# Grouping the transposes and value products of the differential heads in a macaron layer's token mixer

## The chip, the cores and the metric

The kernel runs on one core of one Trainium2 chip. The metric is the time of one execution in microseconds on the device; below it is the median of three runs. One further execution was taken with the hardware profiler. Engines are named as in the profile: PE (TensorE, matrix products), PEld (its weight loads), DVE (VectorE), ACT (ScalarE), POOL (GpSimd) and SP (SyncE, which issues transfers).

## The reference, cut to what matters

A layer of 512 positions and width 1024: half a feed forward, a token mixer, half a feed forward, each behind an RMS norm and added to the input. Half of the mixer's width belongs to four differential heads; the other half to eight dilated heads. The change touches the differential ones:

```python
def diff_attention(q, k, v, lam, bias_table):
    ...
        s = jnp.einsum('bhmqd,bhmkd->bhmqk', q_blk, k).astype(jnp.float32) * scale
        dist = (start + jnp.arange(Q_BLOCK))[:, None] - k_pos[None, :]
        bias = table[t5_bucket(dist)].transpose(2, 0, 1).reshape(H, 2, Q_BLOCK, S)
        s = jnp.where(dist >= 0, s + bias, -jnp.inf)
        p = jax.nn.softmax(s, axis=-1)
        a = p[:, :, 0] - lam * p[:, :, 1]
        return jnp.einsum('bhqk,bhkd->bhqd', a, v32)
...
    oa = diff_attention(qa, ka, va, lam, rel_bias[:, :2 * N_DIFF_HEADS])
    oa = rmsnorm(oa, subln_gain) * (1.0 - lam0)
```

Each differential head has two query/key maps of width 64 and one value of width 128. The queries are taken in four rows of 128; row `i` sees `i + 1` blocks of 128 keys. The second map's probabilities, weighted, are subtracted from the first's, and the result times the values goes through an RMS norm of its own.

## The kernel before, in words

The mixer's order on PE, DVE and ACT is written out by the program itself. The frame is the projections: `plan` lists them (`q0 v0 q1 v1 q2 q3 q4 v2 q5 q6 v3 q7`), each cut into eight chunks. A `q` chunk is six products of 128 x 512 (a slice of the query and key projections of one pair of heads or one head), a `v` chunk twelve of 128 x 256 (values for two heads at a time). Chunk number `t` is called step `t`. `put(t, rank, f)` hangs a piece of attention work on a step: pieces of rank below 10 are issued before that step's chunk, in the order of their ranks, the others behind it. After that, one split of a weight (high part on ACT, low part on DVE) is taken from a list. Nothing is reordered afterwards on these three engines: an instruction that waits holds up everything behind it on its engine.

`attention(u, s)` hangs up one unit of work. Units 0 to 3 are the differential heads, starting at steps 12, 29, 45 and 53; units 4 to 7 are pairs of dilated heads, starting at 61, 77, 85 and 99. For a differential head:

- `score(m, i)` at step s + 2i + m (rank 6): two PE passes into a bank of the tag `s` (two buffers), a DVE instruction that adds the bias strip and takes the extreme (L1061), and `exp` on ACT (L1064).
- `combine(i)` at s + 2i + 3 (rank 5): reciprocal, factor and the weighted sum of the two maps on DVE (L1068 to L1075). It leaves row `i` of the probabilities in `pr`.
- `turn(0, i)` at tv + 2i (rank 2): `i + 1` transposes on PE (L1127) into a bank of the tag `t` (two buffers) and an ACT copy (L1130) into `ptb` (two buffers). Here tv is s + 5 or the step at which the head's values are projected, whichever is later: 17, 34, 50, 58.
- `values(0, i)` at tv + 2i + 2 (rank 1): `i + 1` products (L1139), two records each, into `po`, one of four banks of the tag `mm`, which the projections use too.
- From e = tv + 9 (26, 43, 59, 67): `squares` (e, rank 7; a small DVE instruction and four squares on ACT, L1147), `mean` (e + 1, rank 7; `f` and its successor on DVE, L1155 and L1156), four pieces of an inverse root by Newton steps (e + 2 and e + 3, rank 8, DVE), `scale` (e + 4, rank 7; DVE, L1161 and L1162), `finish` (e + 6, rank 3; four transposes on PE into a bank of the tag `t`, L1168, and an ACT copy), `finish_low` (e + 7, rank 8; the split `ml` on DVE, L1182).

For a dilated unit, `turn_part` (L1094, copy L1105) turns pieces of both maps into a tile of the tag `tx` (one buffer, 3072 columns); rows are scaled by `combine` (L1080 and L1084) at s + 2i + 3, the last at s + 2i + 2. The tag `tx` belongs to the input of the feed forwards outside the mixer and to the dilated units 4 to 6 within it.

What a query projection leaves in its banks is read by DVE (`tq` and `tk`, L970 and L972) and split again by ACT and DVE (L982 to L1008).

Of the kernel before, what the change touches and what calls it, by code (L numbers as in the profile page):

```python
# [14 lines left out]
F32 = mybir.dt.float32  # L15
# [6 lines left out]
P = 128  # L22
S = 512
# [5 lines left out]
NQ = S // P  # L29
# [25 lines left out]
HS = S // 2  # L55
# [4 lines left out]
OFF = [0, 128, 384, 768]  # L60
# [3 lines left out]
def tile_macaron(ctx: ExitStack, tc, xs, xT, wf, wgu1, wst1, wd1, wdg1, wqk, wv, wo, wgu2, wst2, wd2,  # L64
                 wdg2, lams, relb, onehot, addc, out):
    nc = tc.nc
    V, A, G, T = nc.vector, nc.scalar, nc.gpsimd, nc.tensor
# [4 lines left out]
    tp = ctx.enter_context(tc.tile_pool(name="tp", bufs=2))  # L72
    wp = ctx.enter_context(tc.tile_pool(name="wp", bufs=3))
    sp = ctx.enter_context(tc.tile_pool(name="sp", bufs=4))
    pp = ctx.enter_context(tc.tile_pool(name="pp", bufs=4, space=PSUM))
# [5 lines left out]
    def mm_bank(nm):  # L81
        return pp.tile([P, S], F32, tag="mm", name=nm, bufs=4)
# [8 lines left out]
    ident = cp.tile([P, P], F32, tag="ident", name="ident")  # L91
# [642 lines left out]
    with tc.manual_schedule(engines={mybir.EngineType.DVE, mybir.EngineType.Activation}):  # L734
        for t in range(4):
            raw = wp.tile([P, 1024], F32, tag="raw", name=f"raw_f{t}")
            h, l = w_place()
            for kk in range(2):
                k = 2 * t + kk
# [23 lines left out]
                if k > 1:  # L763
                    add_square(k - 1)
                tiles = [(heads[j][i], kk * 512 + (2 * j + i) * P)
                         for j in range(2) for i in range(2)]
                if k == 0:
                    for wx, xx in ((h, early[0]), (h, early[1]), (l, early[0])):
                        for ps, o in tiles:
                            T.matmul(ps[:], wx[:, o:o + P], xx[0][:],  # L770
                                     start=wx is h and xx is early[0], stop=False)
# [99 lines left out]
    v_end = [8 * plan.index(f"v{u // 2}") + 8 for u in range(8)]  # L871
    at = {}

    def put(t, rank, f, *a):
        at.setdefault(t, []).append((rank, f, a))
# [39 lines left out]
    vt = {}  # L915
# [123 lines left out]
    def attention(u, s):  # L1039
        diff, quick = u < 4, u == 7  # L1040
        st = {}
# [78 lines left out]
                             skip_group_check=True)  # L1120
                n += w

        def turn(m, i):
            w = (i + 1) * P
            pt = pp.tile([P, S], F32, tag="t", name=f"pt{u}{m}{i}", bufs=2)
            for k in range(i + 1):
                T.transpose(pt[:, k * P:(k + 1) * P],  # L1127
                            st["pr"][m][:, OFF[i] + k * P:OFF[i] + (k + 1) * P], ident[:])
            ptb = tp.tile([P, S], F32, tag="ptb", name=f"ptb{u}{m}{i}", bufs=2)
            A.copy(ptb[:, :w], pt[:, :w])  # L1130
            st["ptb", m, i] = ptb

        def values(m, i):
            if "po" not in st:
                st["po"] = mm_bank(f"po{u}")
                st["po3"] = st["po"][:].rearrange("p (i d) -> p i d", i=NQ)
            fo = (u % 4) * P
            for k in range(i + 1):
                T.matmul(st["po3"][:, i, :], st["ptb", m, i][:, k * P:(k + 1) * P],  # L1139
                         vt[0, k][:, fo:fo + P], start=k == 0, stop=k == i)  # L1140

        def squares():
            ob_ = tp.tile([P, S], F32, tag="ob", name=f"ob{u}")
# [51 lines left out]
            put(s + step * i + (1 if quick else 3 if diff or i < 3 else 2),  # L1195
                5 if diff or quick or i != 2 else 6.5, combine, i)
        if diff:
            tv = max(s + 5, v_end[u])
            for i in range(NQ):
                put(tv + 2 * i, 2, turn, 0, i)  # L1200
                put(tv + 2 * i + 2, 1, values, 0, i)
            e = tv + 9
            put(e, 7, squares)
            put(e + 1, 7, mean)
            for j in range(4):
                put(e + 2 + j // 2, 8, lambda j=j: st["rs"][j]())
            put(e + 4, 7, scale)
            put(e + 6, 3, finish)
            put(e + 7, 8, finish_low)
        elif quick:  # L1210

            for j, part in enumerate((((0, 0, 3),), ((1, 1, 3), (2, 2, 3)),
                                      tuple((k, 3, 4) for k in range(NQ)))):
                for m in range(2):
                    put(s + 4 + j, 2, turn_part, m, part)
                put(s + 5 + j, 1, values_part, part)
            put(s + 7, 3, finish)
            put(s + 7, 4, finish_low)
        else:
            tv = max(s + 9, v_end[u])  # L1220
            parts = ((0, 0, 4),), ((1, 1, 4),), ((2, 2, 4), (3, 3, 4))
            for j, part in enumerate(parts):
                for m in range(2):
                    put(tv + j, 2, turn_part, m, part)
                put(tv + 4, 1, values_part, part)
            put(tv + 5, 3, finish)
            put(tv + 5, 8, finish_low)

    for w in plan:
        chunks += (qk_chunks if w[0] == "q" else v_chunks)(int(w[1]))  # L1230
        if w[0] == "q":
            attention(int(w[1]), len(chunks) + (4 if w[1] == "0" else 3 if w[1] == "7" else 5))
# [336 lines left out]
```

## Time and profile before

| what | value |
|---|---|
| median of three runs | 931.54 us (931.29 to 931.55) |
| the profiled execution | 932.39 us |
| its span, first to last instruction | 930.6 us |
| mean granted TensorE clock | 0.999 |
| copies of turned probabilities, L1130 | 16, of 255 to 591 ns, median 427 |

The profile gives one execution. The differential heads' attention lies between about 360 and 483 us of the span, the rest of the mixer and the feed forwards around it. In a timeline each row is the start in us, the length in us, the engine, the line, the operation, the tile written and the tiles read, the shape, the count of instructions merged into the row, and in brackets the idle time before it with the instruction that ended it. `L1061` is line 1061 of the kernel before. A length on PE is that of a record, whose end overlaps its successor.

### The profile page before, as it was taken

What the parts mean: (1) busy time and instruction counts of PE and PEld (TensorE: products, weight loads), DVE (VectorE), ACT (ScalarE), POOL (GpSimd) and SP (SyncE); (2) the same over time, 40 slices, a digit from 0 to 9 for tenths busy, and PEclk for the clock granted to TensorE, in tenths of its full rate; (3) what the DMA queues carried; (4) which work ended last, traced back from release to release, by engine and by line L of the source; (5) the groups of instructions that cost most, each with busy time, mean ns of one, the idle gap of its engine ahead of it and who ended that gap; (6) DMA issues with size and microseconds to landing.
All of it is one profiled execution on the core that took longest, in us unless ns stands there. A gap on an engine that the chain in (4) does not pass through costs nothing.

```text
span 930.6 us, 17116 instructions
## 1 busy us (share of the span) xinstructions
PE 922.9 (99%) x6402; PEld 854.7 (92%) x6402; DVE 727.9 (78%) x1504; ACT 543.5 (58%) x1122; POOL 98.3 (11%) x117
## 2 busy tenths in 40 slices
PE   9999999999999999999999999999999999999997
PEld 8888999999999999988979778889999999999997
DVE  7797887677888897668876556797888777888784
ACT  7454665355665575656766664455666455665573
POOL 0001100112202100000000003110120012111000
PEclk9999999999999999999999999999999999999999
DMA  7446646578757562434343213464774678875542
GB/s 260 121 144 154 158 122 177 138 182 210 201 131 207 138 176 94 132 97 129 97 136 92 68 48 133 114 173 102 183 189 120 162 199 193 209 178 153 136 126 91
DMA packets 59876, 136.71 MB, mean 147 GB/s; under 512 B 6848, under 2 KB 8128, under 8 KB 59792
## 3 DMA queue, kind: packets, MB, share of 16 engines
q1 hardware_dynamic: 45792, 110.14, 36.8%
q0 software_dynamic: 14000, 25.47, 17.6%
q8 instruction: 50, 0.82, 0.4%
q14 instruction: 34, 0.28, 0.1%
HBM read 130.30 MB, written 2.14 MB: 142 GB/s over the span
## 4 chain that ended last, share of the span: by engine, by line
PE 97%; DVE 2%; DMA 0%; issue 0%; ACT 0%; DVEq 0%; SPq 0%
PE pv L935 2%; PE pv L933 2%; PE pv L934 2%; PE pq L123 2%; PE pwo L123 2%; PE pq L124 2%; PE pq L125 2%; PE pk L125 2%; PE pk L123 2%; PE pk L124 2%; PE pwo L124 2%; PE pwo L125 2%; PE pua L125 2%; PE pua L124 2%; PE pua L123 2%; PE pda L124 1%
## 5 line engine op out<-in xcount | busy, mean ns | idle before, releaser
L1064 ACT ACTIVATE pr<-pr,mx 128x128 f32<-128x128 f32 (+3 forms) x64 | 36.1, 564 | 34.3 <-DVE mx L1061 34.0
L1061 DVE CUSTOM_DVE_ANT_0 pr<-sc,strip 128x128 f32<-128x128 f32 (+3 forms) x64 | 30.7, 488 | 22.4 <-PE sc L1059 22.0
L391 ACT CAST w<-s2b 128x512 fp32r<-128x512 f32 x50 | 31.1, 621 | 17.1 <-DVE s2b L373 14.8
L395 DVE TENSOR_TENSOR w<-s2b,w 128x512 fp32r<-128x512 f32 x50 | 34.3, 686 | 7.3 <-ACT w L391 7.3
L391 ACT CAST w<-s2a 128x512 fp32r<-128x512 f32 x46 | 28.6, 622 | 17.5 <-DVE s2a L373 14.6
L395 DVE TENSOR_TENSOR w<-s2a,w 128x512 fp32r<-128x512 f32 x46 | 31.5, 686 | 6.6 <-ACT w L391 6.6
L150 POOL TENSOR_TENSOR sq<-sq,sqt 128x512 f32<-128x512 f32 x7 | 10.9, 1564 | 240.2 <-ACT sqt L149 240.1
L933 PE MATMUL pv<-w,xh 128*128 128x256 f32 x128 | 36.2, 283 | 0.0
L935 PE MATMUL pv<-w,xh 128*128 128x256 f32 x128 | 36.2, 283 | 0.0
L934 PE MATMUL pv<-w,xl 128*128 128x256 f32 x128 | 36.2, 282 | 0.0
L123 PE MATMUL pq<-xh,w 128*128 128x512 f32 x64 | 26.3, 410 | 0.0
L123 PE MATMUL pwo<-mh,w 128*128 128x512 f32 x64 | 25.5, 399 | 0.0
L124 PE MATMUL pq<-xl,w 128*128 128x512 f32 x64 | 25.1, 393 | 0.0
L125 PE MATMUL pq<-xh,w 128*128 128x512 f32 x64 | 25.0, 391 | 0.0
L125 PE MATMUL pk<-xh,w 128*128 128x512 f32 x64 | 25.0, 391 | 0.0
L123 PE MATMUL pk<-xh,w 128*128 128x512 f32 x64 | 25.0, 391 | 0.0
L124 PE MATMUL pk<-xl,w 128*128 128x512 f32 x64 | 25.0, 391 | 0.0
L124 PE MATMUL pwo<-ml,w 128*128 128x512 f32 x64 | 25.0, 390 | 0.0
L125 PE MATMUL pwo<-mh,w 128*128 128x512 f32 x64 | 24.9, 390 | 0.0
L934 PEld LDWEIGHTS pv<-w,xl 128*128 128x128 f32 x128 | 24.4, 191 | 0.3
L933 PEld LDWEIGHTS pv<-w,xh 128*128 128x128 f32 x128 | 24.4, 191 | 0.2
L935 PEld LDWEIGHTS pv<-w,xh 128*128 128x128 f32 x128 | 24.5, 191 | 0.0
(709 smaller groups left out, 3997.9 us busy)
## 6 DMA issues: line engine op xcount, KB each, us to landing
raw_qk<-wqk_dram SPq DMA_DIRECT2D x16, 512.0 KB, 3.4
raw0bg<-wst_dram SPq DMA_DIRECT2D x9, 512.0 KB, 4.8
raw_gua<-wgu_dram SPq DMA_DIRECT2D x8, 512.0 KB, 3.5
raw0ag<-wst_dram SPq DMA_DIRECT2D x8, 512.0 KB, 4.7
raw0ad<-wdg_dram SPq DMA_DIRECT2D x8, 512.0 KB, 4.7
strip<-bias_rows SPq DMA_DIRECT2D x16, 256.0 KB, 3.7
raw_v<-wv_dram SPq DMA_DIRECT2D x8, 512.0 KB, 3.3
raw_wo<-wo_dram SPq DMA_DIRECT2D x8, 512.0 KB, 3.3
```

Of the source, the lines that this page charges most:

```text
L123: T.matmul(po, wh, mh, start=first, stop=False, skip_group_check=on)
L124: T.matmul(po, wh, ml, start=False, stop=False, skip_group_check=on)
L125: T.matmul(po, wl, mh, start=False, stop=last, skip_group_check=on)
L150: G.tensor_tensor(sq[:], sq[:], t[:], op=ALU.add)
L391: A.copy(made[t][0], source(t))
L395: V.tensor_tensor(l, source(t), h.bitcast(F32), op=ALU.subtract)
L933: T.matmul(po, xh[k][:, xs], wh[:, o:o + 256], start=k == 0, stop=False)
L934: T.matmul(po, xl[k][:, xs], wh[:, o:o + 256], start=False, stop=False)
L935: T.matmul(po, xh[k][:, xs], wl[:, o:o + 256], start=False, stop=k == KD - 1)
L1061: V.tensor_tensor_reduce(out=pi, in0=ps[:, :w], in1=st["b"][m][:, w - 1::-1], op0=ALU.add, op1=ALU.min, scale=1.0, scalar=3.0e38, accum_ou ...
L1064: A.activation(pi, pi, AF.Exp, scale=-1.0, bias=st["mx"][:, m, i:i + 1], accum_out=st["ls"][:, m, i:i + 1])
```

## The change

The four `turn` events of a differential head become two. Rows 0 and 2 together (four transposes, one bank) and row 1 (two transposes, the other bank) are turned at s + 8; row 3 (four transposes) at s + 10. The copies, of 512, 256 and 512 columns, go into one tile of the tag `tx`, in which `place` records each row's column. All ten value products run in one event at the later of s + 12 and the values' projection, that is at steps 24, 41, 57 and 65. What follows counts from e = tv + 1, which is 25, 42, 58 and 66: one step earlier than before for each head. The first argument of `turn` and `values` that was always 0 goes. Lines below the edit stand up to seven later in the new file (`mean` at L1162 and L1163, `scale` at L1168 and L1169).

```diff
-        def turn(m, i):
-            w = (i + 1) * P
-            pt = pp.tile([P, S], F32, tag="t", name=f"pt{u}{m}{i}", bufs=2)
-            for k in range(i + 1):
-                T.transpose(pt[:, k * P:(k + 1) * P],
-                            st["pr"][m][:, OFF[i] + k * P:OFF[i] + (k + 1) * P], ident[:])
-            ptb = tp.tile([P, S], F32, tag="ptb", name=f"ptb{u}{m}{i}", bufs=2)
-            A.copy(ptb[:, :w], pt[:, :w])
-            st["ptb", m, i] = ptb
-
-        def values(m, i):
-            if "po" not in st:
-                st["po"] = mm_bank(f"po{u}")
-                st["po3"] = st["po"][:].rearrange("p (i d) -> p i d", i=NQ)
+        def turn(tiles):
+
+            if "tx" not in st:
+                st["tx"] = tp.tile([P, 12 * HS], F32, tag="tx", name=f"ptx{u}", bufs=1)
+            for own in tiles:
+                pt = pp.tile([P, S], F32, tag="t", name=f"pt{u}{own[0]}", bufs=2)
+                n, c0 = 0, st.get("used", 0)
+                for i in own:
+                    st["place", i] = c0 + n
+                    for k in range(i + 1):
+                        o = OFF[i] + k * P
+                        T.transpose(pt[:, n:n + P], st["pr"][0][:, o:o + P], ident[:])
+                        n += P
+                A.copy(st["tx"][:, c0:c0 + n], pt[:, :n])
+                st["used"] = c0 + n
+
+        def values():
+            st["po"] = mm_bank(f"po{u}")
+            st["po3"] = st["po"][:].rearrange("p (i d) -> p i d", i=NQ)
             fo = (u % 4) * P
-            for k in range(i + 1):
-                T.matmul(st["po3"][:, i, :], st["ptb", m, i][:, k * P:(k + 1) * P],
-                         vt[0, k][:, fo:fo + P], start=k == 0, stop=k == i)
+            for i in range(NQ):
+                for k in range(i + 1):
+                    o = st["place", i] + k * P
+                    T.matmul(st["po3"][:, i, :], st["tx"][:, o:o + P],
+                             vt[0, k][:, fo:fo + P], start=k == 0, stop=k == i)
...
         if diff:
-            tv = max(s + 5, v_end[u])
-            for i in range(NQ):
-                put(tv + 2 * i, 2, turn, 0, i)
-                put(tv + 2 * i + 2, 1, values, 0, i)
-            e = tv + 9
+            put(s + 8, 2, turn, ((0, 2), (1,)))
+            put(s + 10, 2, turn, ((3,),))
+            tv = max(s + 12, v_end[u])
+            put(tv, 1, values)
+            e = tv + 1
             put(e, 7, squares)
```

## The prediction

> **What bounds the kernel now.** I read the first two parts of the page, then busy time in two stretches of the mixer that hold all four differential heads, then the two lines that the change rewrites.
>
> ```profile
> span 930.6 us, 17116 instructions
> PE 922.9 (99%) x6402; PEld 854.7 (92%) x6402; DVE 727.9 (78%) x1504; ACT 543.5 (58%) x1122; POOL 98.3 (11%) x117
> 360.00:420.00 60.00, 60.00 (x398) 55.04 (x397) 40.44 (x114) 37.53 (x91) 0.00 (x0) 1.00 0.36 108
> 420.00:483.00 63.00, 63.00 (x382) 55.28 (x382) 52.35 (x168) 44.10 (x123) 0.00 (x0) 1.00 0.39 118
> L1127 PE MATMUL pt<-ident,pr x40: 270/272/273, 373.9 to 462.7; 128*128 128x128 f32 x40
> L1139 PE MATMUL po<-v,ptb x80: 270/275/275, 377.6 to 467.4; 128*128 128x128 f32 x80
> ```
>
> In the two rows of windows stand sum and mean, then PE, weight loads, DVE, ACT and POOL, each with its instructions, then the granted clock, DMA share and GB/s. PE is busy in all 123 us at clock 1.00, so the end moves only by what PE executes or waits for. DVE has 52.35 of 63 us in the second stretch: little room for anything late there. The lines give minimum, median and maximum of one record (ns). A record overlaps its successor, so the price of one is the distance to the next start, which the chain of waits (start, length, what ran) shows:
>
> ```profile
> 384.94 0.67 PE po L1139 x6
> 385.61 0.44 PE pt L1127 x4
> 386.05 0.23 PE pq L123
> ```
>
> A record of either kind costs 0.11 us (0.67/6, 0.44/4). The six end exactly where the four begin, and those where the projection begins: the change of kind leaves nothing to see.
>
> **Parts without a price on PE.** The 40 transposes and 80 value records stay, in other places: nothing. Four turns per head become two, four groups of values one; a vanished boundary saves what the chain shows as 0 to 0.01 us, so some 0.1 us for all heads. The upper bound of this gain is the fast rival's, below. ACT has three copies per head for four, of the same elements, on an engine with 44.10 of 63 us used: nothing. SP's and POOL's queues keep their order, and no DMA is added. Everything behind the values (squares, mean, root, scaling, final transposes, split) comes one chunk of projection earlier and moves past what stood there.
>
> **What can be late.** Row 2's probabilities are now turned one chunk after they are combined, where two lay between; so are row 3's. For heads 0 and 1:
>
> ```profile
> 378.24 0.62 DVE L1075 SCALAR_TENSOR_TENSOR pr<-pr,cc,pr 128x384 f32<-128x384 f32 x1
> 379.89 0.39 PE L123 MATMUL pq<-xh,w 128*128 128x512 f32 x1
> 408.49 0.62 DVE L1075 SCALAR_TENSOR_TENSOR pr<-pr,cc,pr 128x384 f32<-128x384 f32 x1
> 410.13 0.39 PE L123 MATMUL pq<-xh,w 128*128 128x512 f32 x1
> ```
>
> Combining ends at 378.86 and 409.11. The matmul behind the new place of the turn begins at 379.89 and 410.13; by then five records of the old order (one transpose, then two value records and two transposes) have not run, so PE comes 5 x 0.11 = 0.55 us earlier, at 379.34 and 409.58. Both are covered by 0.47 us; the cost is nothing, and at most what a delay on DVE of more than 0.47 us leaves.
>
> **Head 2: +0.75 us.**
>
> ```profile
> 428.39 0.69 DVE L1162 TENSOR_TENSOR ob<-po,f 128x512 f32<-128x512 f32 x1
> 428.99 0.68 DVE L970 SCALAR_TENSOR_TENSOR tq<-pq,rbc_n 128x512 f32<-128x512 f32 x1
> 436.14 0.55 DVE L1061 CUSTOM_DVE_ANT_0 pr<-sc,strip 128x384 f32<-128x384 f32 x1
> 436.61 0.75 DVE L1182 SCALAR_TENSOR_TENSOR ml<-ot,sub,mh 128x512 fp32r<-128x512 f32 x1
> 437.28 0.68 DVE L897 TENSOR_TENSOR w<-raw_v,w 128x512 fp32r<-128x512 f32 x1
> 438.94 0.62 DVE L1075 SCALAR_TENSOR_TENSOR pr<-pr,cc,pr 128x384 f32<-128x384 f32 x1
> 436.16 0.38 PE L1139 MATMUL po<-v,ptb 128*128 128x128 f32 x2
> 436.75 0.50 PE L1058 MATMUL sc<-k,q 128*128 128x512 f32 x1
> 438.70 0.32 PE L1058 MATMUL sc<-k,q 128*128 128x256 f32 x1
> ```
>
> The score matmul at 436.75 already waits: the four records before it end at 436.16 + 4 x 0.11 = 436.60, and the bank it wants is read at 436.14 by DVE, which is full here. After the change head 1's scaling (0.60 us to the next start) lies a step earlier, but so does its split `ml` (437.28 − 436.61 = 0.67), now ahead of the read at 436.14. The read therefore stays where it is, the score still starts at about 436.75, and the 0.55 us that PE no longer does before it become wait. Behind it DVE is 0.67 earlier: combining ends at 439.56 − 0.67 = 438.9, while PE is at the turn at 438.70: another 0.2. Sum 0.75. Lower bound: the read comes 0.6 earlier with the scaling, and today's pause of 0.15 goes too (−0.15). Upper: combining does not come earlier (0.55 + 439.56 − 438.70 = 1.4). I take the middle, which follows the queue's order.
>
> **Head 3: +1.3 us.** The nearest thing to a cascade.
>
> ```profile
> 447.12 0.34 PE L1058 MATMUL sc<-k,q 128*128 128x384 f32 x1
> 447.30 0.34 PE L1059 MATMUL sc<-l,q 128*128 128x384 f32 x1
> 448.27 0.56 DVE L1061 CUSTOM_DVE_ANT_0 pr<-sc,strip 128x384 f32<-128x384 f32 x1
> 452.32 0.62 ACT L1064 ACTIVATE pr<-pr,mx 128x384 f32<-128x384 f32 x1 [0.81 <-DVE mx L1061]
> 454.26 0.35 ACT L1147 ACTIVATE ob<-po,cs 128x128 f32<-128x128 f32 x1
> 455.54 0.21 ACT L1147 ACTIVATION_READ_ACCUMULATOR ob<-po,cs 128x1 f32 x1
> 454.01 0.62 DVE L1075 SCALAR_TENSOR_TENSOR pr<-pr,cc,pr 128x384 f32<-128x384 f32 x1
> 455.78 0.22 DVE L1155 SCALAR_TENSOR_TENSOR f<-ss,kapt,cs 128x4 f32<-128x4 f32 x1 [0.40 <-ACT ob L1147]
> 455.90 0.28 PE L1058 MATMUL sc<-k,q 128*128 128x256 f32 x1
> 460.02 0.28 PE L1058 MATMUL sc<-k,q 128*128 128x256 f32 x1
> 474.19 0.16 DVE L158 TENSOR_SCALAR yi_a<-ss 128x4 int32<-128x4 int32 x1
> 474.99 0.16 DVE L164 SCALAR_TENSOR_TENSOR yi_a<-yt_a,yi_a 128x4 f32<-128x4 f32 x1
> ```
>
> The score at 447.12 now has all 20 value records of head 2 before it where it had 12: 447.12 + 0.75 (head 2's pause) + 8 x 0.11 = 448.75. With its second pass (0.18 + 0.34) it is done at 449.3, so DVE's read goes from 448.27 to 449.3: 1.03 later. The row's `exp` on ACT then ends not at 452.94 but at 453.97. Head 2's four squares (454.26 to 455.75: 1.49) now follow directly, to 455.5. `f`, which waits for them (it already shows 0.40 of idle), has moved ahead of the combining of row 2 and holds DVE's queue until 455.55; with its successor 0.5, then 1.1 for the combining (its reciprocal starts 0.46 before the row at 454.01): it ends at 457.15. PE is at the turn at 455.90 + 0.75 − 0.55 = 456.1. Wait 1.05, of which I take 0.95, since PE itself may come up to 0.1 later. Row 3 follows: from 457.15 DVE has to read a 512-wide score (0.7, the 0.55 row's size scaled), start the root (five instructions, 0.2 apart by the rows at 474.19 and 474.99: 0.9 to 1.0), read a 128-wide score (0.3), do six more root instructions (1.2) and combine a row one block wider (1.2): 461.45, while PE, twelve old records short by six, comes at 460.02 + 0.75 + 0.95 − 0.67 = 461.05: 0.35. Sum 1.3. Lower bound 0.3 (DVE makes up the 1.03 in its own gaps), upper 1.6.
>
> **Head 4 (dilated) +0.3, and head 3's transposes +0.5.**
>
> ```profile
> 473.19 0.22 DVE L1155 SCALAR_TENSOR_TENSOR f<-ss,kapt,cs 128x4 f32<-128x4 f32 x1
> 473.79 0.48 DVE L1080 TENSOR_SCALAR pr<-pr,rl 128x512 f32<-128x512 f32 x1
> 474.25 1.03 PE L1094 MATMUL pt<-ident,pr 128*128 128x128 f32 x8
> 478.55 0.82 PE L1094 MATMUL pt<-ident,pr 128*128 128x128 f32 x6
> 479.07 0.86 ACT L1105 COPY ptx<-pt 128x384 f32<-128x384 f32 x2 [1.18 <-PE pt L1094]
> 479.12 0.48 PE L123 MATMUL pq<-xh,w 128*128 128x512 f32 x1
> ```
>
> Ahead of head 4's last scaling (473.79 to 474.27) the first five root instructions (five by 0.2: 1.0) take the place of `f` and its successor (0.45 of the 0.60 between the first two rows). The fourth transpose reads that row at 474.25 + 3 x 0.11 = 474.57, 0.30 after it is ready; 0.55 later is 0.25 to 0.3 too late (bounds 0 and 0.6). The final transposes of head 3 now come directly behind the six at 478.55, which fill both transpose banks; the first is free when ACT's first copy is, at 479.07 + 0.43 = 479.5 or a little later. PE would be there at 479.12: 0.4 to 0.5 (bounds 0 and 0.5).
>
> **The sum.** −0.1 + 0.75 + 1.3 + 0.3 + 0.5 = +2.75 us. Against the profiled execution's 932.39 us (span 930.6 and 1.8 around it) that is 935.1. The median of the runs is 0.85 below that execution: 931.54 + 2.75 = **934.3**. The lower bounds together give about 931.5, the upper ones 935.6.
>
> **Rivals.** (1) *The waits are absorbed.* For it: DVE and ACT work less than PE in every window, so a later start can be made up, and each of my waits is built on the one before it. Against it: DVE's row of 52.35 in 63 us, with the gaps outside the stretches in question. Only head 2 and the transposes remain: −0.1 + 0.75 + 0.5 = +1.15, 932.7. That the whole change only shuffles covered work (931.5) belongs here. (2) *The cascade is longer.* Every wait at its upper bound, and DVE late through head 4: +4 to +5, 936. (3) *Faster: each change of kind has a hidden tail.* Where PE goes from transposes or values back to projections the last record runs to its end: 272 ns less the 0.11 us step is 0.16 us, eight such places vanish, 1.3 us, and the pause of 0.15 at 436.75 goes if the split's place does not matter: 931.54 − 1.45 = 930.1. It decides if the first projection after a turn starts a full record later; the chain above, where 385.61 + 0.44 is 386.05, speaks against it.
>
> The Trainium skill ("TensorE: Matmul & The Clock Gate", Single matmul latency) gives an isolated matmul (398 + N)/2.4 ns, an estimated 219 ns at N = 128, against a gap of N/2.4 + 2.5 in a stream; by that rule a boundary that drained PE would cost an estimated 0.16 us, and rival 3 would hold. The trace agrees with the long record and shows no drain. The same page ("A second HAM failure mode: psum-queue depth-cycling") says that frequent micro-idles of PE between groups of matmuls make its clock oscillate; by that rule my four pauses would cost more than their length.
>
> (4) *The new pauses cost clock.* If each of four pauses halved the clock for 1.7 us, it would add 3 to 4 us to the sum: 938. The row of the second window shows clock 1.00 although the pause at 436.75 lies in it.
>
> **How the numbers follow.** Forecast 0.57 (its own range 933.0 to 936.0), absorbed 0.27, longer cascade 0.09, faster 0.05, clock 0.02. The range 931.5 to 936.6 leaves out the faster and the clock case and the edges of the others, some 0.15. The bound for "the same" is 0.2%, what a measurement of this kernel can tell: 929.7 to 933.4. Below it lies a part of the faster case, 0.03; above it nearly all of forecast, cascade and clock, less the forecast's lower edge: 0.65; the rest, 0.32, is the same.
>
> **What would show it.** PE's timeline: a pause of about 0.8 us before a 512-wide score near 436.7, one of 0.2 at the next turn; about 1 us before head 3's six transposes near 456, with row 2's combining ending just before; 0.3 inside head 4's last eight transposes; 0.5 before head 3's final four. `f` ahead of that combining on DVE, waiting for the squares. Every boundary without a pause shows rival 3 wrong. I am wrong if the waits before heads 2 and 3 are missing, or if a pause stands where no row above lets one be expected, heads 0 and 1 first.

## The result, and the profile after

| | median | runs |
|---|---|---|
| before | 931.54 us | 931.20 to 931.79, 5 runs |
| after | 935.06 us | 934.63 to 935.75, 5 runs |
| ratio after to before | 1.0037 | 95% interval 1.0026 to 1.0048 |
| profiled execution after | 935.75 us, span 934.0 us | before: 932.39 us, span 930.6 us |

The change costs 3.5 us; 2.75 was forecast. Two lines of the page after and two rows of windows that hold the differential heads (sum and mean, then PE, weight loads, DVE, ACT and POOL, then the granted clock, DMA share and GB/s):

```profile
span 934.0 us, 17110 instructions
PE 923.7 (99%) x6402; PEld 854.4 (91%) x6402; DVE 728.2 (78%) x1504; ACT 542.3 (58%) x1118; POOL 98.2 (11%) x117
360.00:420.00 60.00, 60.00 (x398) 54.98 (x396) 41.73 (x117) 37.73 (x89) 0.00 (x0) 1.00 0.38 112
420.00:486.00 66.00, 63.60 (x382) 55.01 (x382) 51.61 (x166) 43.44 (x119) 0.00 (x0) 1.00 0.36 110
```

PE has the same 6402 products, and heads 0 and 1 lie in a window that is still full. In the second stretch, three us longer than its counterpart, PE is idle for 2.4 us. The view of waits says for what (engine and line that waited, what it waited for, us in total, times, longest):

```profile
PE pt L1094 <- DVE pr L1080: 1.0, 1, 1.0
...
PE pt L1134 <- DVE pr L1075: 0.7, 1, 0.7
PE sc L1058 <- DVE mx L1061: 0.5, 1, 0.5
...
PE ot L1175 <- ACT ptx L1105: 0.2, 1, 0.2
```

These are four waits at four places; the view of before had none of them. They count idle time from the end of the last record. As records overlap, a start is delayed by more. I take that delay from PE's timeline, as the distance of two starts less the distance without a wait:

```profile
436.73 0.50 PE L1058 MATMUL sc<-k,q 128*128 128x512 f32 x1 [0.49 <-DVE mx L1061]
437.07 0.39 PE L1059 MATMUL sc<-l,q 128*128 128x512 f32 x1
...
438.69 1.02 PE L1134 MATMUL pt<-ident,pr 128*128 128x128 f32 x6
439.46 0.36 PE L1058 MATMUL sc<-k,q 128*128 128x256 f32 x1
...
442.54 0.39 PE L125 MATMUL pk<-xh,w 128*128 128x512 f32 x1
442.84 0.63 PE L1134 MATMUL pt<-ident,pr 128*128 128x128 f32 x4
443.23 0.36 PE L1058 MATMUL sc<-k,q 128*128 128x256 f32 x1
...
456.16 0.27 PE L1134 MATMUL pt<-ident,pr 128*128 128x128 f32 x1
457.10 0.76 PE L1134 MATMUL pt<-ident,pr 128*128 128x128 f32 x5 [0.67 <-DVE pr L1075]
...
460.93 0.28 PE L935 MATMUL pv<-w,xh 128*128 128x256 f32 x1
461.11 0.63 PE L1134 MATMUL pt<-ident,pr 128*128 128x128 f32 x4
461.49 0.36 PE L1058 MATMUL sc<-k,q 128*128 128x256 f32 x1
...
465.31 2.39 PE L1146 MATMUL po<-v,ptx 128*128 128x128 f32 x20
467.46 0.42 PE L1058 MATMUL sc<-k,q 128*128 128x384 f32 x1
...
476.00 0.49 PE L1094 MATMUL pt<-ident,pr 128*128 128x128 f32 x3
477.49 0.77 PE L1094 MATMUL pt<-ident,pr 128*128 128x128 f32 x5 [1.00 <-DVE pr L1080]
...
481.51 0.82 PE L1094 MATMUL pt<-ident,pr 128*128 128x128 f32 x6
482.57 0.66 PE L1175 MATMUL ot<-ident,ob 128*128 128x128 f32 x4 [0.24 <-ACT ptx L1105]
```

For head 3, 457.10 − 456.16 − 0.11 = 0.83 us; for head 4, 477.49 − 476.00 − 3 x 0.11 = 1.16; for head 3's final transposes, 482.57 − 481.51 − 6 x 0.11 = 0.40. The six transposes of head 2 take 439.46 − 438.69 = 0.77 to the next score instead of 0.66, 0.1 to 0.15 of waiting; its last score starts 0.65 late (0.49 of idle and the overlap), where before it was 0.15 late. Two more waits are too short for the view to list. Row 3 of head 2 starts 0.30 us after the product ahead of it, where 0.23 is the step without a wait, and its four transposes take 0.39 to the next score instead of 0.36: 0.10 us. Row 3 of head 3 starts after 0.18 instead of 0.12 and takes 0.38 instead of 0.35: 0.09 us. (The steps without a wait are those of the versions below in which these rows are ready in time.) Sum of the new waits: 0.50 + 0.14 + 0.10 + 0.83 + 0.09 + 1.16 + 0.40 = 3.2 us. The span grew by 3.4. The rest stands behind the waits. Six transposes that wait for nothing take 0.57 to the next product (479.47 to 480.04), so five take 0.46; the five at 457.10 and the five at 477.49 take 0.52, and the six of head 2 took 0.20 more than 0.57, not 0.14. Some 0.06 us behind each of these three waits brings the sum to 3.4.

Behind the largest wait stands a chain on DVE and ACT. DVE's timeline after, at head 4:

```profile
468.09 0.56 DVE L1061 CUSTOM_DVE_ANT_0 pr<-sc,strip 128x384 f32<-128x384 f32 x1 [2.93 <-PE sc L1059]
...
473.29 0.22 DVE L1162 SCALAR_TENSOR_TENSOR f<-ss,kapt,cs 128x4 f32<-128x4 f32 x1 [0.82 <-ACT ob L1154]
...
476.94 0.49 DVE L1080 TENSOR_SCALAR pr<-pr,rl 128x512 f32<-128x512 f32 x1
```

DVE idles for 2.93 us until a score that stands behind 20 value records. Before, it read that score earlier:

```profile
465.42 0.56 DVE L1061 CUSTOM_DVE_ANT_0 pr<-sc,strip 128x384 f32<-128x384 f32 x1 [1.13 <-PE sc L1059]
```

It was done with the last scaling at 474.27, and after the change at 477.43. That is 3.2 us later, of which PE itself is late by only 1.75 (476.00 against 474.25).

### The profile page after: what moved, and what is told of

Same layout as the page of the kernel before. It is cut to its first block, busy times and chain, and to the rows that moved or that the text cites. A ratio compares the mean times of both kernels' runs of the same rounds, so it can differ in the third digit from the quotient of the medians.

```text
span 934.0 us, 17110 instructions
## 1 busy us (share of the span) xinstructions
PE 923.7 (99%) x6402; PEld 854.4 (91%) x6402; DVE 728.2 (78%) x1504; ACT 542.3 (58%) x1118; POOL 98.2 (11%) x117
## 4 chain that ended last, share of the span: by engine, by line
PE 94%; DVE 4%; ACT 1%; issue 1%; DMA 0%; DVEq 0%; SPq 0%
PE pwo L123 2%; PE pwo L124 2%; PE pwo L125 2%; PE pua L123 2%; PE pua L125 2%; PE pua L124 2%; PE pv L935 1%; PE pv L934 1%; PE pv L933 1%; PE pq L123 1%; PE pk L123 1%; PE pq L124 1%; PE pq L125 1%; PE pk L125 1%; PE pk L124 1%; PE pda L124 1%
```

## The experiments

Twelve edits of the changed kernel, each timed in five rounds beside the kernel before. In the table, the delay at each place is taken as above. "Shift" is the start of one and the same product late in the span (near 919 us of the kernel before), in this trace less in that of before, less the same difference at 350 us, ahead of all the changed work: the growth that one trace shows, free of the start of the span.

| version | median, before beside it | ratio, 95% | shift | head 2 score, turn | head 3 turn | head 4 turn | head 3 final |
|---|---|---|---|---|---|---|---|
| the change | 935.06, 931.54 | 1.0026 to 1.0048 | 3.36 | 0.65, 0.14 | 0.83 | 1.17 | 0.41 |
| `mean` behind the combining | 934.45, 931.86 | 1.0019 to 1.0042 | 2.85 | 0.65, 0.14 | 0 | 1.56 | 0.41 |
| values behind the score | 933.38, 931.86 | 1.0008 to 1.0026 | 1.66 | 0.65, 0.14 | 0 | 0.44 | 0.41 |
| tail one step later | 933.67, 931.86 | 1.0011 to 1.0028 | 1.60 | 0.72, 0.80 | 0 | 0 | 0 |
| three edits | 933.34, 931.86 | 1.0009 to 1.0027 | 1.67 | 0.71, 0.15 | 0 | 0.83 | 0 |
| turns as before, one event of values | 932.25, 931.66 | 0.9998 to 1.0017 | 0.34 | 0.35, 0 | 0 | 0 | 0 |
| late turns alone | 933.79, 931.66 | 1.0014 to 1.0033 | 1.98 | 0.73, 0.81 | 0 | 0 | 0 |
| all one step later | 932.12, 931.66 | 0.9997 to 1.0015 | 0.54 | 0.74, 0 | 0 | 0 | 0 |
| tail by head | 932.79, 931.79 | 0.9999 to 1.0018 | 0.80 | 0.70, 0.15 | 0 | 0 | 0 |
| head 1's tail away | 932.28, 931.79 | 0.9992 to 1.0009 | 0.25 | 0.48, 0 | 0 | 0 | 0 |
| one event more | 932.21, 931.79 | 0.9993 to 1.0010 | 0.60 | 0.75, 0 | 0 | 0 | 0 |
| early rows | 933.64, 931.76 | 1.0012 to 1.0030 | 1.78 | 0, 1.95 | 0 | 0 | 0 |
| early rows, head 1's tail away | 933.41, 931.76 | 1.0007 to 1.0025 | 1.58 | 0, 1.71 | 0 | 0 | 0 |

For "turns as before", 0.35 is the sum of 0.21 ahead of the transposes and 0.14 ahead of the score. The score of head 2 was 0.15 late in the kernel before already. The waits of 0.1 us at row 3 of heads 2 and 3 are not in the table.

**`mean` behind the combining.**

```diff
-            put(e + 1, 7, mean)
+            put(e + 2, 5.5, mean)
```

> Theory Q (a queue order on DVE): `f`, which waits for the four squares, stands ahead of the combining of the next head's row 2 and holds it. With `mean` put behind that combining (e + 2, rank 5.5), head 3's wait of 0.83 us goes, and most of head 4's 1.17 us (to about 0.3); heads 2's pauses and the 0.4 us before the final transposes of head 3 stay: 935.06 - 1.7 = 933.4. Rival S (the late score): what delays the combining is the score that stands behind all the value records, so the waits stay and the time is 934.9 to 935.1. Rival G (the grouping itself costs, through the one tile or the larger copies): 935.1.

Head 3's wait went, as theory Q says. Head 4's grew to 1.56 instead of falling to 0.3, so the median fell by 0.6 instead of 1.7. DVE's timeline of this version at head 4:

```profile
471.73 0.69 DVE L897 TENSOR_TENSOR w<-raw_qk,w 128x512 fp32r<-128x512 f32 x1 [1.33 <-ACT w L893]
472.34 0.22 DVE L1162 SCALAR_TENSOR_TENSOR f<-ss,kapt,cs 128x4 f32<-128x4 f32 x1
```

With `f` out of the way, the next instruction in DVE's queue, the low part of a weight, waits: its high part is cast on ACT behind the same four squares. At head 4, what holds DVE is the squares' place on ACT, and `f` only happened to be the first to ask. There is a slip of mine besides: a dilated unit combines row 2 at rank 6.5, so rank 5.5 put `mean` ahead of a score's read and of that combining, not behind it. Theory Q falls for head 4 and holds for head 3. In its place stands theory A: the wait comes from the late score and from the squares, which stand on ACT ahead of the next `exp` and cast.

**The values behind the score.**

```diff
-            put(tv, 1, values)
+            put(tv, 6.5, values)
```

> The value products run behind the score of their step instead of ahead of it (rank 6.5). Theory Q with the late score as its start: DVE reads head 3's score at about 448.4 instead of 449.4, squares and `f` come about 0.9 us earlier, head 3's wait falls from 0.83 to about 0.1, head 4's from 1.17 to about 0.45: 933.6. If only the place of `f` mattered and not when the squares start: unchanged, 935.1. Rival G: 935.1.

Measured 933.38, with waits of 0 and 0.44 at heads 3 and 4: the size that was expected from the late score. PE and DVE at head 4:

```profile
463.50 0.33 PE L1058 MATMUL sc<-k,q 128*128 128x384 f32 x1
463.68 0.34 PE L1059 MATMUL sc<-l,q 128*128 128x384 f32 x1
463.85 2.39 PE L1146 MATMUL po<-v,ptx 128*128 128x128 f32 x20
```

```profile
464.05 0.56 DVE L1061 CUSTOM_DVE_ANT_0 pr<-sc,strip 128x384 f32<-128x384 f32 x1 [0.69 <-PE sc L1059]
...
470.76 0.23 DVE L1162 SCALAR_TENSOR_TENSOR f<-ss,kapt,cs 128x4 f32<-128x4 f32 x1 [0.20 <-ACT ob L1154]
```

The 20 records are the same 2.15 us of PE work; put behind the score they no longer stand ahead of DVE. Its idle time before the read falls from 2.93 to 0.69, and `f`'s from 0.82 to 0.20. The order within one step is worth 1.7 us of the 3.36.

**The tail one step later** (everything behind the values at its steps of before).

```diff
-            e = tv + 1
+            e = tv + 2
```

> Turns and values stay as in the changed kernel; everything behind the values goes back to the steps that it had before. Theory Q: the waits of head 3 (0.83), head 4 (1.17) and before head 3's final transposes (0.4) go; head 2 keeps the 0.65 before its score and its turn waits longer (its combining is no longer 0.67 earlier, about 0.7 more): 935.06 - 2.4 + 0.7 = 933.0 to 933.4. Rival G: 935.1. If the late turns alone are the cause: 935.1 or more.

Measured 933.67, 0.3 above the expected range, with the places as expected: the three waits gone, head 2's turn at 0.80. One place was not expected: at head 1, row 3 is combined at 413.21 and its turn starts at 413.35, 0.15 late. PE's timeline at head 2:

```profile
437.18 0.50 PE L1058 MATMUL sc<-k,q 128*128 128x512 f32 x1 [0.56 <-DVE mx L1061]
...
439.12 0.27 PE L1134 MATMUL pt<-ident,pr 128*128 128x128 f32 x1
440.03 0.77 PE L1134 MATMUL pt<-ident,pr 128*128 128x128 f32 x5 [0.64 <-DVE pr L1075]
```

The value records still stand ahead of the scores here, and heads 3 and 4 have no wait: the late score costs PE only together with the earlier tail behind it, and taking back either one removes all or most of it. At head 2 the earlier tail is a help: with it the combining comes 0.67 us earlier, as the split `ml` no longer stands between a read and it.

**Three edits at once**: the first two, and the final transposes of head 3 one step later.

```diff
+            late = 1 if u == 3 else 0
-            put(e + 6, 3, finish)
-            put(e + 7, 8, finish_low)
+            put(e + 6 + late, 3, finish)
+            put(e + 7 + late, 8, finish_low)
```

> Three edits at once: `mean` behind the combining, values behind the score, and the final transposes of head 3 one step later. Theory Q: only head 2's pauses are left, 0.65 + 0.11 + 0.14 less the 0.26 that was there before: about 0.6 over the kernel before, 932.2. Rival G: 935 less at most the 0.4 of the final transposes, 934.7.

A miss: 933.34 and not 932.2. The final transposes lost their 0.41, but `mean` at rank 5.5 took 0.4 back at head 4 (0.83, against 0.44 with the values alone). Edits that each help do not add up when they share a queue.

**Parts of the change alone.** In both versions `values` takes the rows that it is to do (that part of the edit is left out here). First, one event of values and the one tile, with the turns and the tail as before:

```diff
-            put(s + 8, 2, turn, ((0, 2), (1,)))
-            put(s + 10, 2, turn, ((3,),))
-            tv = max(s + 12, v_end[u])
-            put(tv, 1, values)
-            e = tv + 1
+            tv = max(s + 5, v_end[u])
+            for i in range(NQ):
+                put(tv + 2 * i, 2, turn, ((i,),))
+            put(tv + 8, 1, values, range(NQ))
+            e = tv + 9
```

> The turns go back to the four steps that they had before (but into the one tile); the values stay in one event, at the step of the last one of before, and the tail is where it was before. Theory Q: grouping the values and keeping them in one tile has no price of its own but some 0.2 us more pause before head 2's last score, since two records less stand before it: 931.5 to 931.9. Rival G: most of the 3.5 us stays, 934 or more.

Measured 932.25, 0.35 above the expected range, with an interval that holds no change; the shift is 0.34. Keeping the turned rows in the one tile and grouping the values have no price beyond 0.2 us more at head 2's last score and some 0.1 us spread over heads 0 and 1. Rival G falls. Then the late turns alone, with the values row by row and the tail as before:

```diff
             put(s + 8, 2, turn, ((0, 2), (1,)))
             put(s + 10, 2, turn, ((3,),))
-            tv = max(s + 12, v_end[u])
-            put(tv, 1, values)
-            e = tv + 1
+            tv = max(s + 5, v_end[u])
+            for i in range(NQ):
+                put(max(tv + 2 * i + 2, s + 9 + i), 1, values, (i,))
+            e = tv + 9
```

> The turns stay where the change puts them (two events, s + 8 and s + 10); the values go row by row as soon as they can and the tail is where it was before. Theory Q: only head 2 loses, 0.55 us of cover before its last score and about 0.85 at its turn, since its combining ends at 439.56 as before: 1.4 over the kernel before, 932.9. If the late turns alone make the whole loss: 935. If they cost nothing: 931.5.

Measured 933.79, 0.9 above the expectation by the median and 0.6 by the shift. Head 2's two waits are 0.73 and 0.81 as expected; a row of values one step behind its turn adds a wait of 0.24 for ACT's copy, which I had not counted; head 1 grows by 0.18, as in the version with the tail later, and row 3 of head 2 waits 0.1.

**All one step later**, with the values behind the score:

```diff
-            put(s + 8, 2, turn, ((0, 2), (1,)))
-            put(s + 10, 2, turn, ((3,),))
-            tv = max(s + 12, v_end[u])
-            put(tv, 1, values)
+            put(s + 9, 2, turn, ((0, 2), (1,)))
+            put(s + 11, 2, turn, ((3,),))
+            tv = max(s + 13, v_end[u])
+            put(tv, 6.5, values)
```

> The change with turns and values one step later (s + 9, s + 11, s + 13), the values behind the score, so that the tail stands where it did before and two steps lie between combining and turning again. Theory Q: the only price left is the cover before head 2's last score, 0.55 us: 932.0; nothing faster than the kernel before by more than 0.3. Rival G: 935.

Measured 932.12: one chunk more between combining and turning, and the tail at its old steps, and only head 2's score still waits:

```profile
435.94 0.50 PE L1058 MATMUL sc<-k,q 128*128 128x512 f32 x1 [0.57 <-DVE mx L1061]
```

**The tail by head**: the changed kernel with the values behind the score and the tail later for heads 2 and 3 only.

```diff
-            put(tv, 1, values)
-            e = tv + 1
+            put(tv, 6.5, values)
+            e = tv + (1 if u < 2 else 2)
```

> The change's turns and values event stay at their steps, the values behind the score; the tail goes one step later (to its steps of before) for heads 2 and 3 alone. Theory A (after the first runs: head 4's wait comes from ACT, where head 3's squares stand ahead of the next exp, and from the late score, whatever the place of f): the waits of heads 3 and 4 and before the final transposes all go, and only head 2's pauses are left, 0.55 over the kernel before (932.2 to 932.4). If the late turns themselves cost something at heads 3 and 4: 0.3 to 0.8 more.

The three waits are gone, as theory A says. The median, 932.79, is 0.4 above the expected and would fit the rival as well; the shift, 0.80, and the trace decide. All of the 0.80 lies at head 2: 0.55 at the score, 0.15 at the turn and 0.10 at row 3, of which the expectation had the first alone. With the turns at the change's own steps, late turns cost nothing at heads 3 and 4.

**Head 1's tail away** from the stretch in which DVE is full (on top of "all one step later"):

```diff
+            late = 7 if u == 1 else 0
-            put(e + 4, 7, scale)
-            put(e + 6, 3, finish)
-            put(e + 7, 8, finish_low)
+            put(e + 4 + late, 7, scale)
+            put(e + 6 + late, 3, finish)
+            put(e + 7 + late, 8, finish_low)
```

> The version with everything one step later, in which head 1's scaling, final transposes and split also go seven steps later, out of the stretch in which DVE is full. Theory D (head 2's last score waits because DVE, full with head 1's tail, reads the bank late): that wait falls from 0.74 to 0.1 or less, and the time to 0.1 to 0.2 under the kernel before: 931.3 to 931.7, too near to tell from it by the median. Rival (the bank's read waits for its own score, or for ACT): the wait stays and the time is that of the version without this edit, 932.1.

Half right. The wait fell from 0.74 to 0.48, not to 0.1:

```profile
435.03 0.50 PE L1058 MATMUL sc<-k,q 128*128 128x512 f32 x1 [0.32 <-DVE mx L1061]
```

DVE's timeline of this version shows why:

```profile
426.80 0.42 DVE L1061 CUSTOM_DVE_ANT_0 pr<-sc,strip 128x256 f32<-128x256 f32 x1
427.14 0.08 DVE L1061 DVE_READ_ACCUMULATOR2_ANT mx<- 128x1 f32 x1
427.16 0.69 DVE L970 SCALAR_TENSOR_TENSOR tq<-pq,rbc_n 128x512 f32<-128x512 f32 x1
...
434.41 0.55 DVE L1061 CUSTOM_DVE_ANT_0 pr<-sc,strip 128x384 f32<-128x384 f32 x1
```

DVE has caught up by 427.16, where it takes over a projection as it ends (PE's last product into `pq` ends at 427.13); from there to the read at 434.41 it runs its own order without a gap of more than 0.05 us. I put what is left of the wait down to this projection's own work for DVE; no run takes that work away. The median, 932.28, lies above the expected 931.3 to 931.7, at a ratio of 1.0000 to the kernel before; the shift is 0.25.

**One event more** (on top of "all one step later"):

```diff
-            put(s + 9, 2, turn, ((0, 2), (1,)))
+            put(s + 8, 2, turn, ((1,),))
+            put(s + 9, 2, turn, ((0, 2),))
```

> The version with everything one step later, in which row 1 is turned in an event of its own one step ahead: one event more for each head. If a boundary between transposes and projections costs what the chain shows (0 to 0.01 us): the same as without it, 932.1. By the rule of a drained tail, 0.16 us for each of the eight changes of kind: 0.65 to 1.3 more.

The shift goes from 0.54 to 0.60: eight changes of kind more cost 0.06 us together. They cost what the chain of waits showed before, and grouping could win no more.

**Early rows** (on top of "all one step later"), and the same with head 1's tail away:

```diff
-            put(s + 9, 2, turn, ((0, 2), (1,)))
+            put(s + 6, 2, turn, ((0, 1),))
+            put(s + 9, 2, turn, ((2,),))
```

> The version with everything one step later, in which rows 0 and 1 (three transposes) are turned at s + 6, ahead of head 2's last score, and row 2 alone at s + 9. Theory C (part of head 2's loss is work that no longer stands ahead of a score which must wait anyway): three transposes of 0.11 us fill 0.33 of the 0.74 us of wait: 0.41 is left, and the time falls by 0.3 from that of the version without the edit, to 0.1 to 0.2 over the kernel before: 931.8 to 932.0. Rival: the wait moves with the work put ahead of it, 0.74 stays and the time is 932.1 to 932.2.

> The same, with head 1's scaling, final transposes and split seven steps later as well: the candidate for a version that beats both kernels. Theory: the wait of 0.48 us that this second edit alone left falls to about 0.15, and the span lies 0 to 0.2 us under that of the kernel before; the median can't be told from 931.8. More than 0.5 under it would mean that the grouping saves something that I have not found.

Both missed, on the slow side by 1.6 us. PE's timeline of the first:

```profile
433.08 0.27 PE L1134 MATMUL pt<-ident,pr 128*128 128x128 f32 x1
435.14 0.44 PE L1134 MATMUL pt<-ident,pr 128*128 128x128 f32 x2 [1.79 <-DVE pr L1075]
435.33 0.48 PE L1058 MATMUL sc<-k,q 128*128 128x512 f32 x1
```

Row 1 is combined a step before this turn in the order of the program, but DVE is some 2 us behind PE in this stretch. The wait for the score was swallowed by a longer one for the combining. I had counted steps and not looked up when that combining ends in the version it was put on. No version here beats the kernel before; the nearest is equal to it.

## Why the prediction was right, and where it was not

**What bounds the kernel, and the parts without a price.** Right: PE's products are the same, heads 0 and 1 cost nothing (the product at 432 us of the kernel before is 0.03 us later after the change, as it already was at 350), and boundaries are worth 0.06 us for eight. The window with all four listed waits has a granted clock of 1.00, so the clock rival did not come.

The run with one event more shows 0.008 us for each change of kind. The Trainium skill ("TensorE: Matmul & The Clock Gate", Single matmul latency) would by its isolated latency at N = 128, less the 56 ns between two starts that the page gives for matmuls back to back, make it an estimated 0.16 us if PE drained there. Both figures are for bf16; for a stream in which each matmul has a weight load of its own, as here, the same page of the Trainium skill gives about 81 ns, which would make the estimate 0.14. The run shows about a twentieth of either: PE does not drain there.

By the same page of the Trainium skill ("A second HAM failure mode: psum-queue depth-cycling"), PE idling often between groups of matmuls makes its clock oscillate, in a bf16 kernel. The few waits here left it at 1.00.

**Head 2: +0.75.** Right in place and mechanism. In DVE's timeline after, the read stayed where it was (436.14 before):

```profile
436.12 0.55 DVE L1061 CUSTOM_DVE_ANT_0 pr<-sc,strip 128x384 f32<-128x384 f32 x1
```

The score started at 436.73. Measured 0.64: 0.50 and 0.14 (0.20 by the start of the next product). Another 0.10 came at row 3, which I had priced for head 3 alone. The two versions with the change's turns and the tail at its old steps show the predicted upper bound of the second part, 0.8.

**Head 3: +1.3.** The chain was right link by link, and the runs with the score first and with the tail later each undo it. The links after the change, on DVE and ACT:

```profile
449.39 0.56 DVE L1061 CUSTOM_DVE_ANT_0 pr<-sc,strip 128x384 f32<-128x384 f32 x1 [1.19 <-PE sc L1059]
...
455.58 0.22 DVE L1162 SCALAR_TENSOR_TENSOR f<-ss,kapt,cs 128x4 f32<-128x4 f32 x1 [0.83 <-ACT ob L1154]
...
456.42 0.62 DVE L1075 SCALAR_TENSOR_TENSOR pr<-pr,cc,pr 128x384 f32<-128x384 f32 x1
...
460.21 0.75 DVE L1075 SCALAR_TENSOR_TENSOR pr<-pr,cc,pr 128x512 f32<-128x512 f32 x1
```

```profile
453.44 0.62 ACT L1064 ACTIVATE pr<-pr,mx 128x384 f32<-128x384 f32 x1 [1.65 <-DVE mx L1061]
453.96 0.19 ACT L1064 ACTIVATION_READ_ACCUMULATOR pr<-pr,mx 128x1 f32 x1
454.06 0.35 ACT L1154 ACTIVATE ob<-po,cs 128x128 f32<-128x128 f32 x1
```

Against my 449.3, 455.55 and 457.15 stand 449.39, 455.58 and 457.04. The turn waited 0.83 (predicted 0.95). Of the further 0.35 at row 3 only 0.09 came: I summed the lengths of the pieces from 457.15 to 461.45, 4.3 us, but from the end of row 2's combining to that of row 3's it is 3.9 (457.04 to 460.96), since neighbours on DVE overlap too. Head 3 was over-counted: 0.92 in place of 1.3.

**Head 4: +0.3, the step that was mis-sized.** It measured 1.17, outside its bounds of 0 and 0.6. I priced there only the root's instructions that took the place of `f`, and left out that head 3's 20 value records stand ahead of head 4's score in just the same way as head 2's ahead of head 3's. I had worked out that chain for head 3 and did not repeat it. Its parts are in the rows above: the read at 468.09 and the squares that hold `f` for 0.82. The score first leaves 0.44 there, the tail later leaves nothing.

**Head 3's final transposes: +0.5.** Right: 0.41, for the first copy of the two that had filled both banks.

**The sum and the rivals.** −0.1 + 0.74 + 0.92 + 1.17 + 0.41 is 3.14 with the measured waits (the −0.1 as predicted), 3.3 with the 0.06 behind three of them; 2.75 was predicted, and the trace shows 3.36. That the predicted sum came so near is in part luck: the 0.38 too much at head 3 and the 0.87 too little at head 4 partly made up for each other. Of the rivals, the absorbed waits did not come: of the places that I priced, DVE had made up its delay only at head 3's row 3, and there not quite. The longer cascade came at head 4, by one link, not through the whole of it.

## What to carry to other kernels

A group of work put ahead of another engine's input can cost that engine the length of the group, though nothing is added where it runs (here DVE idled 2.24 us less once 2.15 us of records stood behind the score): put the piece that others wait for first, and the group behind it. When an order is moved by a step, work out the chain once for every place where the pattern recurs, and look up in the trace when the producer ends; a distance counted in steps says nothing where an engine is two us behind. A queue's wait belongs to what is late (here the squares on ACT), not to the instruction that waits first: moved away, it leaves the next one waiting.

## What the runs showed of the hardware beyond that

Going from transposes to projections and back cost 0.06 us for eight more changes, though each transpose's record is 272 ns long and starts are 110 ns apart. A score that had to wait behind a projection pays a little more than its wait: from 436.73 to its second pass at 437.07 it takes 0.34 us where 0.23 is usual. Where a row of probabilities was ready only just before PE came, its transposes still started 0.15 us behind the end of the combining (442.69 to 442.84 at head 2, 460.96 to 461.11 at head 3), so a row that was ready 0.1 us ahead of PE still held it.
